# Folding the maxima to 64 partitions on VectorE before they are transposed

## The chip, the cores and the metric

The kernel runs on one NeuronCore of a Trainium2 chip. The metric is the device time of one execution in microseconds (us). Three executions of the kernel before took 636.18, 636.55 and 637.14 us; their median, 636.55 us, is the time before.

A word on the engines, as the profile names them: PE is TensorE (its weight loads are listed apart, as PEld), DVE is VectorE, ACT is ScalarE, POOL is GpSimd, SP is SyncE, which here issues most DMAs. Each works off its own queue in order; semaphores tie them together.

## What is computed

One layer of a diffusion backbone for 1024 tokens of width 1024, and 256 context tokens. A normalised, modulated input goes through one projection; half of its columns feed a neighbourhood attention (8 heads of 64, a clamped window of 8 by 16 grid cells and a learned bias, with all 256 context keys in the same softmax), the other half a gated short convolution; one output projection follows. The change touches the softmax of the attention alone:

```
s_lat = einsum(q_rot, k_rows) * scale + bias        # masked outside the window
s_ctx = einsum(q_plain, kc) * scale
s = concatenate([s_lat, s_ctx], axis=-1)
p = softmax(s, axis=-1)
o = einsum(p_lat, v_rows) + einsum(p_ctx, vc)
```

The softmax subtracts a maximum over all keys of a query. That maximum is what the changed lines work out.

## The kernel before

The kernel has four parts: the modulation and the normalised input (to about 78 us), the projection of queries, keys and values (to about 265 us), the attention, and the output projection (from about 533 us). The change lies in the attention.

**How the attention is tiled.** Scores are kept transposed, with the keys on the 128 partitions and the queries along the free dimension. Queries come in 8 blocks of 128, keys likewise; a block j of keys meets the query blocks j - 1 to j + 1, up to 384 columns. The 256 context keys are two further blocks. The loop at the end calls `quarter(n)` for n from 0 to 35: four quarters for each of the eight heads, each with 256 queries, and some more to let the pipeline run empty. A quarter works at three depths at once: it takes the scores of quarter n, the exponentials of quarter e = n - 2, and the product with the values of quarter o = n - 3.

**The maximum of a query.** `mx` is one tile of 128 partitions by 1024 queries. `ctx_max` (L992) writes the maximum of the two context blocks into the 256 columns of a quarter, `lat_max` (L1007) takes the maximum with the biased scores `sb` of a key block, in place, twice a quarter. After that each column of `mx` holds 128 partial maxima, one for each partition. They are brought together over the partitions two quarters after their scores, in `quarter` (L1082 to L1097): TensorE transposes the two blocks of 128 columns into a PSUM tile `pm` (`pmx` in the profile), VectorE reduces each over its 128 elements to `rm`, one number for each query; TensorE transposes `rm`, broadcast, back into the other half of `pm`, and ScalarE copies that to `mg`, where all partitions hold the maximum of each query. `ctx_exp` (L1030) and L1111 subtract `mg` from the scores `sc` and `sb`; the exponentials and their low parts (`phc`, `plc`, `phl`, `pll`) follow.

**What sets the order.** From the list `strict` on, every instruction on TensorE, ScalarE, VectorE and GpSimd is chained behind the one issued before it on its engine, so that the attention's instructions stand just as the program writes them. Between the attention's own matmuls TensorE runs fillers: matmuls of the gates and of the convolution (`pu`), handed out in ticks by the table `TICKS`. On VectorE, the splits `ul` of the filler's weights, the gates and the convolution's products stand between `rm` and `sc`, where the maximum is on its way through TensorE and ScalarE. So a quarter on VectorE reads: `rm`, fillers' work, `sc`, `sb` less `mg`, the new `sb` with its bias, `mx` from context, `mx` twice from `sb`, `pll`; then the next quarter's `rm`. On TensorE: the pair of transposes of `mx`, the context's product with the values (`po`, six matmuls), the pair of transposes of `rm`, the scores `pss` and `pc`, fillers, `po` of the window, fillers.

Almost every instruction passes through one helper, so the profile shows L55 for them and they are told apart by their tiles.

Of the kernel before, what the change touches and what calls it, by code (L numbers as in the profile page):

```python
# [14 lines left out]
ALU = mybir.AluOpType  # L15
AX = mybir.AxisListType
# [3 lines left out]
P = 128  # L20
# [19 lines left out]
def body(tc, es, x, ctxt, w_ada, b_ada, w_in, q_g, k_g, rpbr, w_out, vecs, cst, out):  # L40
# [21 lines left out]
    pe, act, dve, pool = every = [ordered(e) for e in (nc.tensor, nc.scalar, nc.vector, nc.gpsimd)]  # L62
# [50 lines left out]
    ident = ci[:, 0:P]  # L113
# [196 lines left out]
    def do_acts():  # L310
        for c in soon + (slow if not any(c[1] and c[1].__name__ == "product" for c in soon) else []):
            if c[0]:
                c[0]()
                c[0] = None

    def do_dves(most=99):
        for queue in chores:
            while queue and not queue[0][0] and (queue is soon or most > 0 and not soon):
                on_dve = queue.pop(0)[1]
                if on_dve:  # L320
                    on_dve()
                    most -= 1
# [481 lines left out]
    for m in range(1, 4):  # L804
        k, new, last = 2 * m, m < 3, m == 3
# [247 lines left out]
    def pair_of(n):  # L1053

        h, g = divmod(n, 4)
        two = [(h, 0), (h - 1, 7)] if g == 0 else [(h, 2 * g - 1), (h, 2 * g)]
        return [(i, heads[h_], j) for i, (h_, j) in enumerate(two) if 0 <= h_ < NH]

    def both(v, n, pair):

        w = 256 if n % 4 == 0 else 384
        return v[:, pair[0][0]:pair[-1][0] + 1, :w]

    def maxima_of(n, pair):

        step, w = (768, 256) if n % 4 == 0 else (P, 384)
        lo = (2 * (n % 4) - 2) * P if n % 4 else pair[0][0] * step
        v = mg[:, lo:lo + w].rearrange("p (o c) -> p o c", o=1)
        if len(pair) == 1:
            return v  # L1070
        part = list(v.ap)
        return bass.AP(v.tensor, v.offset, [part[0], [step, 2], [1, w]])

    def quarter(n):

        live = lambda m: 0 <= m < 4 * NH
        ticks = TICKS[n]  # L1080
        e, o = n - 2, n - 3
        if live(e):  # L1082
            hd, g = heads[e // 4], e % 4
            pm = psm.tile([P, 512], F32, name="pmx", tag="C", bufs=2)
            for i in range(2):
                pe.transpose(pm[:, i * P:(i + 1) * P], mx[:, (2 * g + i) * P:(2 * g + i + 1) * P], ident)
            rm = ap.tile([P, 2], F32, name="rm", tag="rm", bufs=8)
            dve.tensor_reduce(rm, pm[:, :256].rearrange("p (i k) -> p i k", i=2), AX.X, ALU.max)
        if live(o):
            heads[o // 4].ctx_out(o % 4)  # L1090
        do_dves(3)
        if gating and next(gating[0], "end"):
            gating.pop(0)
        if live(e):
            for i in range(2):
                pe.transpose(pm[:, 256 + i * P:256 + (i + 1) * P], rm[:, i:i + 1].broadcast_to([P, P]), ident)
            act.copy(mg[:, g * 256:(g + 1) * 256], pm[:, 256:512])  # L1097
        now = pair_of(n)
        for i, hd_, j in now:
            hd_.scores(j, sbank[:, i])  # L1100
        if n == 0:
            next(fill)
            ticks -= 1
        if live(n):
            heads[n // 4].ctx_scores(n % 4)
        if live(e):
            hd.ctx_exp(g)
        if e in sbs or e in exps:
            pair, sb = pair_of(e), sbs.pop(e)
            w = both(sb, e, pair)  # L1110
            dve.tensor_tensor(w, w, maxima_of(e, pair), ALU.subtract)  # L1111
            exps[e] = [ap.tile([P, 2, 384], F32R, name=m, tag=m, bufs=2) for m in ("phl", "pll")]
            ph, pl = (both(v, e, pair) for v in exps[e])
            act.activation(ph, w, AF.Exp)
            act.activation(w, w, AF.Exp)
        for _ in range(n > 0):
            next(fill, None)
        done = []
        if o >= 0:
            pho, plo = exps.pop(o)  # L1120
            for i, hd_, j in pair_of(o):
                hd_.lat_out(j, pho[:, i], plo[:, i])
                if j in (4, 7):
                    done.append((hd_, j // 7))
                    if j == 7 and hd_.s:
                        ready.append(hd_.p)
        if now:
            sb = sbs[n] = sb_new()
            g_ = n % 4
            if g_:  # L1130
                bt = now[0][1].bt
                bias = bt[:, 1:2].broadcast_to([P, 2, 384]) if g_ == 2 else bt[:, 0:2] if g_ == 1 else bt[:, 1:3]
                dve.tensor_tensor(sb, sbank[:, :, :384], bias, ALU.add)
            else:
                for i, hd_, j in now:
                    cols = slice(P, 384) if j == 0 else slice(0, 256)
                    dve.tensor_tensor(sb[:, i, :256], sbank[:, i, :256], hd_.bt[:, 1, cols], ALU.add)
            if live(n):
                heads[n // 4].ctx_max(n % 4)
            for i, hd_, j in now:  # L1140
                hd_.lat_max(j, sb[:, i])
        if e in sbs or e in exps:
            dve.tensor_tensor(pl, w, ph.bitcast(F32), ALU.subtract)
        for _ in range(ticks - (n > 0)):
            next(fill, None)
        for hd_, bank_ in done:
            hd_.finish(bank_)
        do_acts()
# [36 lines left out]
    for n in range(NT + 3):  # L1185


        p, t = divmod(n, NB)
# [119 lines left out]
    with sbuf("att") as ap, psum("psb") as psb:  # L1308
        sbank = psb.tile([P, 2, 512], F32, name="pss")
        strict[:] = every  # L1310
        mx = ap.tile([P, T], F32, name="mx")
# [3 lines left out]
        for n in range(4 * NH + 4):  # L1315
            h, g = divmod(n, 4)
            if 0 < h < NH and g == 0:
                heads[h].load_v()
            if h + 1 < NH and g:
                nx = heads[h + 1]  # L1320
                for load in ((nx.masks, nx.load_q), (nx.load_k,), ())[g - 1]:
                    load()
            quarter(n)
            if ready:
                p = ready.pop()
                if p < NPAIR - 1:
                    gating.append(gated(p))
                else:
                    recip(p, ap)
# [149 lines left out]
```

## Time and profile before

| | us |
|---|---|
| median of three runs | 636.55 |
| the profiled execution, by the device | 636.67 |
| its span, first to last instruction | 634.9 |
| PE busy in the span | 627.2 |
| DVE busy in the span | 443.2 |
| the reduces `rm` start, first and last of 32 | 279.0 and 513.6 |

The page and the views are of one execution. A row of the timeline gives start, duration, engine, line, operation, output<-inputs, shape (partitions x elements; for a matmul rows*columns of the weights, then what is moved) and count; what stands in square brackets is idle time of the engine just before, and what ended it. A row of the grouped view gives, behind the shapes and the count, busy time and mean duration in ns, then the idle time before the group and its releasers. In the view of one tile the three numbers behind the count are the shortest, median and longest duration in ns. Instructions of one engine overlap a little, so the time from one start to the next can be shorter than a duration.

### The profile page before, as it was taken

How to read it: one execution, taken by the hardware profiler on the slowest of the kernel's cores; microseconds unless marked ns; L12 is line 12 of the kernel's file. 1: busy time of each engine (PE TensorE's matmuls, PEld its weight loads, DVE VectorE, ACT ScalarE, POOL GpSimd, SP SyncE). 2: the span in 40 equal slices, each digit the busy share in tenths (PEclk: the TensorE clock that was granted, in tenths of full speed). 3: DMA queues.
4: the chain of work that ended last, by engine and by line, in shares of the span. 5: the costliest groups of instructions: out<-in, count | busy, mean ns of one | idle time of the engine just before them, and what ended most of it. 6: DMA issues, size and time to landing. Idle time of an engine off the chain costs nothing.

```text
span 634.9 us, 10080 instructions
## 1 busy us (share of the span) xinstructions
PE 627.2 (99%) x3503; PEld 538.8 (85%) x3504; DVE 443.2 (70%) x827; ACT 324.0 (51%) x699; POOL 122.5 (19%) x133
## 2 busy tenths in 40 slices
PE   8999999999999999999999999999999999999998
PEld 3477899999899999888888888888888888888787
DVE  1677858765766845468898889988998964476411
ACT  4676835424624545345576658567775854352000
POOL 1305014123123221101122111111111111002400
DMA  8972638867784994875383636583742233965721
GB/s 322 384 260 97 181 114 263 252 198 219 243 264 137 302 330 159 302 246 177 118 273 114 230 109 205 187 284 101 251 146 75 59 103 117 299 212 177 254 101 50
DMA packets 103007, 125.61 MB, mean 198 GB/s; under 512 B 9665, under 2 KB 71577, under 8 KB 101676
## 3 DMA queue, kind: packets, MB, share of 16 engines
q1 hardware_dynamic: 96492, 113.38, 53.7%
q10 hardware_dynamic: 6208, 11.05, 5.5%
q0 software_dynamic: 256, 0.54, 0.4%
q8 instruction: 27, 0.44, 0.3%
q14 instruction: 24, 0.20, 0.1%
HBM read 88.09 MB, written 38.62 MB: 200 GB/s over the span
## 4 chain that ended last, share of the span: by engine, by line
PE 81%; DVE 9%; DMA 5%; ACT 2%; issue 1%; POOL 0%; ACTq 0%; DVEq 0%; POOLq 0%
PE pu L55 23%; PE pacc L55 21%; PE po L55 7%; PE acc L55 6%; PE tr L55 5%; PE cacc L55 4%; PE pss L55 3%; DMA woraw<-in_w_out 2%; PE pmx L55 2%; DVE mx L55 2%; PE pout L75 2%; PE pout L76 2%; PE pout L74 2%; DMA tb<-y_d 2%; PE pc L55 2%; DVE sb L55 2%
## 5 line engine op out<-in xcount | busy, mean ns | idle before, releaser
L55 PE MATMUL pu<-h,uh 128*128 128x512 f32 x544 | 169.2, 392 | 0.0
L55 PE MATMUL pacc<-wh,h 128*128 128x384 f32 x512 | 135.3, 338 | 0.0
L55 PEld LDWEIGHTS pu<-h,uh 128*128 128x128 f32 x544 | 98.2, 188 | 16.9
L55 PE MATMUL pu<-h,ul 128*128 128x512 f32 x272 | 106.4, 391 | 0.0
L55 PEld LDWEIGHTS pacc<-wh,h 128*128 128x128 f32 x512 | 92.9, 188 | 0.1
L55 PE MATMUL pacc<-wl,h 128*128 128x384 f32 x256 | 85.7, 335 | 0.0
L55 POOL TENSOR_TENSOR plc<-sc,phc 128x512 fp32r<-128x512 f32 x32 | 43.0, 1345 | 215.7 <-ACT sc L55 159.1
L55 POOL TENSOR_TENSOR ss<-ss,few 128x4 f32<-128x4 f32 (+1 forms) x40 | 41.4, 1037 | 126.3 <-DVE ss L55 126.1
L55 DVE TENSOR_TENSOR mx<-mx,sb 128x384 f32<-128x384 f32 (+1 forms) x64 | 59.4, 937 | 2.0
L55 PEld LDWEIGHTS pu<-h,ul 128*128 128x128 f32 x272 | 51.1, 188 | 11.2
L75 PE MATMUL pout<-wol,yh 128*128 128x512 f32 (+1 forms) x136 | 51.4, 378 | 0.2 <-DVE wol L1358 0.2
L76 PE MATMUL pout<-woh,yl 128*128 128x512 f32 (+1 forms) x136 | 50.8, 377 | 0.0
L74 PE MATMUL pout<-woh,yh 128*128 128x512 f32 (+1 forms) x136 | 49.9, 378 | 0.0
L55 PEld LDWEIGHTS pacc<-wl,h 128*128 128x128 f32 x256 | 48.2, 188 | 0.1
L55 DVE TENSOR_REDUCE ss<-sq 128x4 f32<-128x260 f32 (+1 forms) x40 | 15.7, 394 | 42.2 <-ACT sq L55 42.2
L55 ACT ACTIVATE sq<-pacc 128x256 f32<-128x256 f32 x32 | 12.3, 384 | 54.7 <-PE pacc L55 54.2
L55 ACT COPY mg<-pmx 128x256 f32<-128x256 f32 x32 | 11.9, 372 | 52.0 <-PE pmx L55 45.6
L55 ACT COPY sc<-pc 128x512 f32<-128x512 f32 x32 | 18.8, 588 | 25.6 <-PE pc L55 25.6
L55 DVE TENSOR_TENSOR pll<-sb,phl 128x768 fp32r<-128x768 f32 (+2 forms) x33 | 28.4, 861 | 4.5 <-ACT sb L55 4.5
L55 ACT ACTIVATE qn<-pacc,ss 128x64 f32<-128x64 f32 x128 | 30.0, 329 | 3.0 <-issue 2.5
L55 PE MATMUL po<-phl,v 128*65 128x256 f32 (+2 forms) x160 | 31.3, 291 | 0.0
L75 PEld LDWEIGHTS pout<-wol,yh 128*128 128x128 f32 x136 | 25.6, 188 | 5.3 <-DVE wol L1358 0.6
(156 smaller groups left out, 1259.5 us busy)
## 6 DMA issues: line engine op xcount, KB each, us to landing
uraw<-in_w_in SPq DMA_DIRECT2D x34, 256.0 KB
q_d<-qs SPq DMA_DIRECT2D x32, 256.0 KB
k_s<-k_d SPq DMA_DIRECT2D x8, 1024.0 KB
q_s<-q_d SPq DMA_DIRECT2D x16, 512.0 KB
wr<-in_w_in SPq DMA_DIRECT2D x40, 192.0 KB
slab<-in_w_ada SPq DMA_DIRECT2D x6, 1024.0 KB
v_d<-vs SPq DMA_DIRECT2D x20, 260.0 KB
v<-v_d SPq DMA_DIRECT2D x16, 325.0 KB
```

The lines of the kernel that those rows point to most:

```text
L55: i = emit(*a, **kw)
L74: i = pe.matmul(ps, ah, bh, start=first, stop=False)
L75: pe.matmul(ps, ah, bl, start=False, stop=False)
L76: pe.matmul(ps, al, bh, start=False, stop=last)
```

## The change

The two transposes of `mx` read 64 partitions instead of 128, with a 64 by 64 corner of the identity, and write 64 columns each; the reduce reads 2 by 64 elements instead of 2 by 128 for each partition. For that, a new instruction on VectorE, at the end of the maxima of each quarter n, takes the 256 columns of the quarter before, whose maxima are complete by then, and writes the larger of partitions 0 to 63 and 64 to 127 into partitions 0 to 63, in place.

```diff
             for i in range(2):
-                pe.transpose(pm[:, i * P:(i + 1) * P], mx[:, (2 * g + i) * P:(2 * g + i + 1) * P], ident)
+                pe.transpose(pm[:, i * 64:(i + 1) * 64], mx[0:64, (2 * g + i) * P:(2 * g + i + 1) * P], ident[:64, :64])
             rm = ap.tile([P, 2], F32, name="rm", tag="rm", bufs=8)
-            dve.tensor_reduce(rm, pm[:, :256].rearrange("p (i k) -> p i k", i=2), AX.X, ALU.max)
+            dve.tensor_reduce(rm, pm[:, :P].rearrange("p (i k) -> p i k", i=2), AX.X, ALU.max)
...
             for i, hd_, j in now:
                 hd_.lat_max(j, sb[:, i])
+        if live(n - 1):
+            low, high = (mx[64 * i:64 * i + 64, (n - 1) % 4 * 256:(n - 1) % 4 * 256 + 256] for i in range(2))
+            dve.tensor_tensor(low, low, high, ALU.max)
         if e in sbs or e in exps:
             dve.tensor_tensor(pl, w, ph.bitcast(F32), ALU.subtract)
```

The built program shows where the new instruction falls. On DVE, this is one quarter of the loop before, from one reduce to the next (a row gives the operation, the tiles, the shape of the output, and the semaphores that it waits for):

```order
L55 TENSOR_REDUCE rm<-pmx 128x2 [waits PE_49]
L55 TENSOR_TENSOR ul<-uraw,uh 128x512 [waits DMAHW7_49,Activation_49]
L55 TENSOR_TENSOR ul<-uraw,uh 128x512 [waits DMAHW2_49,Activation_49]
L55 TENSOR_TENSOR sc<-sc,mg 128x512 [waits Activation_49,Pool_49]
L55 TENSOR_TENSOR sb<-sb,mg 128x768
L55 TENSOR_TENSOR sb<-pss,bt 128x768 [waits DVE_49,PE_49]
L55 TENSOR_TENSOR mx<-pc,sc 128x256 [waits Activation_49]
L55 TENSOR_TENSOR mx<-mx,sb 128x384 [waits DVE_49] x2
L55 TENSOR_TENSOR pll<-sb,phl 128x768 [waits Activation_49]
L55 TENSOR_REDUCE rm<-pmx 128x2 [waits PE_49]
```

And the end of the same quarter in the changed program:

```order
L55 TENSOR_TENSOR sb<-pss,bt 128x768 [waits DVE_49,PE_49]
L55 TENSOR_TENSOR mx<-pc,sc 128x256 [waits Activation_49]
L55 TENSOR_TENSOR mx<-mx,sb 128x384 [waits DVE_49] x2
L55 TENSOR_TENSOR mx<-mx 64x256 [waits DVE_49]
L55 TENSOR_TENSOR pll<-sb,phl 128x768 [waits DVE_49,Activation_49]
L55 TENSOR_REDUCE rm<-pmx 128x2 [waits PE_49]
```

The new maximum stands between the second `mx` from `sb` and `pll`, and both it and `pll` now wait for the DVE instruction before them.

On PE, the piece of the difference that holds the transposes of one quarter and what follows them:

```order
-L55 MATMUL pmx<-ci,mx 128x128 [waits DVE_49,Activation_49]
-L55 MATMUL pmx<-ci,mx 128x128 [waits DVE_49]
+L55 MATMUL pmx<-ci,mx 128x64 [waits DVE_49,Activation_49]
+L55 MATMUL pmx<-ci,mx 128x64
 L55 MATMUL pmx<-ci,rm 128x128 [waits DVE_49]
 L55 MATMUL pmx<-ci,rm 128x128
```

The transposes stay where they were and wait for DVE as before, the first of the pair for both; that of `rm` is unchanged. No other instruction moves on any engine.

## The prediction

> **What bounds the kernel now.** I read the page's busy times first, then the stage that the change touches, then its waits, then one quarter of it in order of time.
>
> ```profile
> span 634.9 us, 10080 instructions
> PE 627.2 (99%) x3503; PEld 538.8 (85%) x3504; DVE 443.2 (70%) x827; ACT 324.0 (51%) x699; POOL 122.5 (19%) x133
> L55 PE MATMUL pmx<-ci,mx x64: 269/272/328, 278.5 to 513.3; 128*128 128x128 f32 x64
> 273.00:516.00 243.00, 241.12 (x1388) 205.09 (x1388) 213.75 (x321) 156.47 (x261) 41.95 (x37) 1.00 0.51 167
> ```
>
> The second line says TensorE (PE) is busy 99% of the span. The third, from the view of the tile pmx, says that the 64 transposes to be shortened run from 278.5 to 513.3 us, two in each of 32 quarters of the attention loop. The fourth is that stretch alone (columns: stretch, length, busy time of PE, PEld, DVE, ACT, POOL, granted clock, DMA share, GB/s): PE is busy 241.1 of 243 us, VectorE (DVE) 213.75, at full clock. So DVE has 29.3 us idle, 0.9 us a quarter. That average doesn't decide; what counts is whether the idle time lies where the new instruction goes. The waits of the stage:
>
> ```profile
> L55 DVE TENSOR_REDUCE rm<-pmx 128x2 f32<-128x256 f32 x32 | 13.5, 423 | 13.3 <-PE pmx L55 13.0
> L55 DVE TENSOR_TENSOR sc<-sc,mg 128x512 f32<-128x512 f32 x32 | 21.9, 685 | 9.8 <-ACT mg L55 9.8
> L55 DVE TENSOR_TENSOR ul<-uraw,uh 128x512 fp32r<-128x512 f32 x25 | 16.8, 684 | 1.9 <-ACT uh L55 1.9
>   PE pmx L55: 13.0, 16
>   DVE rm L55: 4.2, 12
> ```
>
> In a group's row the last part is DVE's idle time ahead of it and its releaser. The last two lines are of the view of the tile rm: its reduce waited for PE in 16 quarters, 13.0 us together, and 12 of the records of PE and PEld waited for the reduce, 4.2 us. In 16 quarters, then, PE sets the pace and DVE has 0.81 us to spare at the reduce; in the other 16 DVE arrives at it without a pause. This is one of the latter:
>
> ```profile
> 347.21 0.42 DVE L55 TENSOR_TENSOR mx<-pc,sc 128x256 f32<-128x256 f32 x1
> 347.66 2.07 DVE L55 TENSOR_TENSOR mx<-mx,sb 128x384 f32<-128x384 f32 x2
> 349.65 0.95 DVE L55 TENSOR_TENSOR pll<-sb,phl 128x768 fp32r<-128x768 f32 x1
> 350.09 0.38 PE L55 MATMUL pmx<-ci,mx 128*128 128x128 f32 x2
> 350.52 0.42 DVE L55 TENSOR_REDUCE rm<-pmx 128x2 f32<-128x256 f32 x1
> 350.89 0.28 PE L55 MATMUL po<-plc,v 128*65 128x256 f32 x1
> 351.01 0.42 PE L55 MATMUL pmx<-ci,rm 128*128 128x128 f32 x2
> 351.46 0.37 ACT L55 COPY mg<-pmx 128x256 f32<-128x256 f32 x1 [1.60 <-PE pmx L55]
> 351.94 0.69 DVE L55 TENSOR_TENSOR sc<-sc,mg 128x512 f32<-128x512 f32 x1 [1.00 <-ACT mg L55]
> 352.55 0.95 DVE L55 TENSOR_TENSOR sb<-sb,mg 128x768 f32<-128x768 f32 x1
> ```
>
> It is a ring. DVE runs from sc through sb, the sums, the maxima (mx) and pll to the reduce (rm) without a gap; the reduce releases PE's second pair of transposes, those ACT's copy mg, that DVE's next sc. The 1.00 us before sc is no spare time: it is the way through PE and ACT, and moves along when the reduce comes late. PE's second pair starts at 351.01, when the reduce has been over for 0.07 us (350.52 + 0.42 = 350.94). Whatever delays the reduce by more than that stops PE, and PE, busy throughout, has nowhere to regain it.
>
> **The change, part by part.** Added, 32 times: a maximum of 64 partitions by 256 elements on DVE, between the last mx and pll, ahead of the reduce. No row has 64 partitions, or two inputs that start on different partitions. The nearest is the same operation on 256 elements in all partitions, mx<-pc,sc, 0.42 us. I take that, since it has the same elements for each partition. Around it lie waits. The order of the changed program shows the maximum waiting for the mx before it, and pll, which so far didn't wait for DVE, waiting for the maximum. Today pll starts before mx is over: 347.66 + 2.07 = 349.73 against 349.65, so 0.08 us of overlap is lost. A DVE instruction that waits for the one before starts 0.03 us after its end (347.21 + 0.42 = 347.63, then 347.66). Together 0.08 + 0.03 + 0.42 + 0.03 = 0.56 us more before pll, and before the reduce.
>
> [...]
>
> Shortened: the reduce reads 128 elements instead of 256. Its nearest row has 130:
>
> ```profile
> L55 DVE TENSOR_REDUCE ss<-sq 128x2 f32<-128x130 f32 x8 | 2.3, 289 | 15.3 <-ACT sq L55 15.3
> 14.36 0.41 PE L55 MATMUL tr<-ci,rw 2*128 2x2 f32 x4 [0.23 <-DVE xss L55]
> L55 PE MATMUL tr<-ci,rw x16: 194/198/222, 14.4 to 62.1; 2*128 2x2 f32 x8, 4*128 4x4 f32 x8
> ```
>
> 423 - 289 = 134 ns, so 0.14 us off (a little more for 128). The ring grows by 0.56 - 0.14 = 0.42 us a quarter on DVE.
>
> Shortened too: each first transpose moves 64 columns instead of 128. Today two follow each other in 0.38 - 0.27 = 0.11 us. The bound from below is a transpose of 2 columns: four take 0.41 us and one 0.20, so (0.41 - 0.20) / 3 = 0.07 us each. Half of 0.11 is 0.055, under that bound; I take 0.07. That gives 0.04 us a transpose, 0.08 a quarter.
>
> [...]
>
> Now the quarters. Sixteen have the reduce straight behind pll: each passes 0.42 us on to PE, 16 × 0.42 = 6.7 us. They don't feel the shorter transposes. Of the sixteen with idle time five have 0.26 to 0.36 us, 1.5 us together; these are the first and the last:
>
> ```profile
> 285.41 0.42 DVE L55 TENSOR_REDUCE rm<-pmx 128x2 f32<-128x256 f32 x1 [0.36 <-PE pmx L55]
> 427.42 0.42 DVE L55 TENSOR_REDUCE rm<-pmx 128x2 f32<-128x256 f32 x1 [0.27 <-PE pmx L55]
> ```
>
> They pay 5 × 0.42 - 1.5 = 0.6 us. The other eleven hide it all in DVE's idle time (13.0 - 1.5 = 11.5 us, about 1 us each), and there PE gains 0.08 us: -0.9 us. Were that cover gone, they would pay 11 × 0.42 = 4.6 us more. Last, DVE's 1.9 us ahead of ul (waiting for ACT's uh, not for the ring) can take up lateness: -1.9 us, if all of it lies in late quarters. Sum: 6.7 + 0.6 - 0.9 - 1.9 = 4.5 us.
>
> ACT, POOL and SP get nothing new, and no DMA moves. What lies behind a late reduce is named above: PE's transposes, and behind them on PE the scores pss and pc and all fillers; so ACT's mg and DVE's sc are late next. POOL stops DVE's maxima for a moment today,
>
> ```profile
> 347.43 1.30 POOL L55 TENSOR_TENSOR plc<-sc,phc 128x512 fp32r<-128x512 f32 x1 [5.94 <-PE po L55]
> ```
>
> but plc ends at 348.73, and the two mx (2.07 us for two that take 1.15 in 275.73) at 349.73, so the new maximum starts clear of it.
>
> ```profile
> 275.73 1.15 DVE L55 TENSOR_TENSOR mx<-mx,sb 128x384 f32<-128x384 f32 x2
> ```
>
> Bounds for the price that no row shows. From below: 0.29 us, the row of 130 elements, as if half the partitions took half the time. The ring then grows by 0.29, and 16 × 0.29 - 16 × 0.08 - 1.9 = +1.4 us. From above: 0.69 us, the row of 512 elements (sc), as if the two halves were read one after the other. The ring grows by 0.69, and 11.0 + (5 × 0.69 - 1.5) - 0.9 - 1.9 = +10.2 us.
>
> The profiled execution took 636.67 us by the device (span 634.9 and 1.8 around it), 0.1 over the median of 636.55. 636.67 + 4.5 = 641.2; against the median 641.0.
>
> **The rivals.**
>
> *The cover holds (faster).* DVE's 29.3 us of idle time exceed 32 × 0.42 = 13.4 us, and PE, the busiest engine, loses 32 × 0.08 = 2.6 us of work: 634.0. For it: PE waits for the reduce only 4.2 us in the whole stage. Against it: the quarter at 347 us, where DVE pauses nowhere but in the ring's way through PE and ACT. It decides if the maximum costs the ring less than the 0.07 us that PE has at its second pair, which no row suggests.
>
> *A wash.* The maximum at its lower bound, +1.4 us, with somewhat more lateness taken up by ACT's and PE's queues: 637.2, in reach of what counts as no change. For it: 64 partitions are half of every row seen. Against it: all DVE rows go by elements a partition (256: 0.42, 512: 0.69, 768: 0.95).
>
> *DVE becomes the bound.* At the upper bound, or if the eleven covered quarters lose their cover because every quarter begins late: 641.0 + 4.6 = 645.6, up to 636.6 + 10.2 = 646.8. For it: a late quarter begins the next one late. Against it: lateness that comes through PE moves PE and DVE alike and leaves the idle time before the reduce as it is.
>
> That the change doesn't do what it says is excluded as far as the order goes: 32 maxima are there, and 64 transposes write 64 columns.
>
> **How the numbers follow.** Forecast, DVE's ring lengthened where DVE arrives last, 639.0 to 643.5 by itself: 0.68. A wash: 0.14. Cover holds: 0.08. DVE the bound: 0.10. A measurement of this kernel tells about 0.2%, 1.3 us, from no change, so under 635.3 is faster and over 637.8 slower. Slower: 0.68 + 0.10 + a fifth of the wash, 0.81. Same: 0.11. Faster: 0.08. For 8 in 10 the range goes from 637.2 (the wash, all below left out) to 645.0 (most of the third rival left out).
>
> **What would show it.** Right: mx<-mx 64x256 at 0.42 us, and pll starting 0.03 us after it; rm at 0.29 us; two transposes in 0.07 us; DVE's wait for pmx before the reduce well under 13.0 us, PE's waits for rm above 4.2 us and in more than 12 records. The quarters with 0.6 us and more of idle time keep their length, those without grow by about 0.4. Wrong: PE's waits for rm unchanged (cover held), a maximum far from 0.42 us, or one stretched by plc; a shift that arises outside 279 to 516 us.

## The result, and the profile after

Four executions of the changed kernel took 645.5 us in the median (644.83 to 646.01), four of the kernel before beside them 636.61 us (636.18 to 637.14): the ratio is 1.0139, interval 1.0126 to 1.0151. The kernel became slower, as forecast, by 8.9 us where 4.5 were forecast, and 0.5 us beyond the top of the range. The profiled execution is the fastest of the four, 644.83 us, 8.2 us over the profiled one of before.

The page of the changed kernel starts with span and busy times; behind the dots are three stretches, the middle one being the attention (columns as before: stretch, length, busy time of PE, PEld, DVE, ACT, POOL, granted clock, DMA share, GB/s).

```profile
span 643.0 us, 10142 instructions
PE 632.6 (98%) x3503; PEld 536.3 (83%) x3504; DVE 457.4 (71%) x859; ACT 324.3 (50%) x699; POOL 122.2 (19%) x133
...
0.00:273.00 273.00, 270.45 (x1575) 237.44 (x1577) 175.16 (x428) 137.07 (x389) 63.67 (x81) 1.00 0.72 237
273.00:525.00 252.00, 247.20 (x1390) 202.73 (x1389) 227.44 (x353) 156.58 (x261) 42.35 (x37) 1.00 0.50 162
525.00:643.00 118.00, 114.94 (x543) 96.11 (x540) 54.77 (x80) 30.62 (x50) 16.22 (x15) 1.00 0.49 169
```

The two outer stretches of the kernel before:

```profile
0.00:273.00 273.00, 270.42 (x1576) 237.70 (x1578) 175.45 (x428) 136.82 (x389) 63.73 (x81) 1.00 0.72 238
516.00:634.90 118.90, 115.63 (x543) 95.97 (x541) 53.98 (x80) 30.67 (x50) 16.78 (x15) 1.00 0.51 168
```

Until 273 us the two agree. The attention went from 243.0 to 252.0 us, the rest from 118.9 to 118.0. The clock is full in all of them. So the whole loss arises where the change lies. DVE has 13.7 us more to do there (227.44 against 213.75). But PE is busy 6.1 us longer too (247.20 against 241.12), with transposes that were to be shorter, and idle 2.9 us longer (252.00 - 247.20 = 4.8 against 1.9).

The waits of the stage, by group and, in the last two lines, by the tile rm:

```profile
L55 DVE TENSOR_TENSOR ul<-uraw,uh 128x512 fp32r<-128x512 f32 x25 | 16.8, 684 | 1.5 <-ACT uh L55 1.5
L55 DVE TENSOR_TENSOR mx<-mx 64x256 f32<-64x256 f32 x32 | 16.5, 517 | 1.1
L55 DVE TENSOR_REDUCE rm<-pmx 128x2 f32<-128x128 f32 x32 | 9.2, 287 | 5.4 <-PE pmx L55 5.3
  PE pmx L55: 5.3, 8
  DVE rm L55: 4.5, 15
```

The reduce waits for PE in 8 quarters and 5.3 us, where it did in 16 and 13.0: the new maximum (the fold, from here on) has used up the idle time. The records that wait for the reduce went from 12 and 4.2 us to 15 and 4.5, the idle time ahead of ul from 1.9 to 1.5. Almost nothing of this looks like 8.9 us, since a ring that turns more slowly shows its waits in no single place.

One wait has become longer. These are the groups of the first transposes, before and after:

```profile
L55 PE MATMUL pmx<-ci,mx 128*128 128x128 f32 x64 | 12.7, 275 | 0.7 <-DVE mx L55 0.7
L55 PE MATMUL pmx<-ci,mx 64*128 64x64 f32 x64 | 10.3, 240 | 4.2 <-DVE mx L55 2.1 <-ACT z L55 0.7 <-ACT ob L55 0.7
```

PE's idle time ahead of them grew from 0.7 to 4.2 us. They wait for DVE as before, but for a later instruction: until now for the maxima of the turn, now for the fold behind them. In the quarter of the prediction the last of these maxima was over at 349.73 us, and the pair started at 350.09 without a pause; after, the fold is over at 353.44 and the pair starts at 353.59. That isn't what makes the reduce of this quarter late: it follows pll at 354.42 without idle time, is over at 354.70, and the second pair starts at 354.76, 0.06 us behind it where it was 0.07. What the longer wait costs elsewhere, no run isolates.

The length of the ring is read better from the start of one reduce to the start of the next. Reduces around the quarter of the prediction, before and after:

```profile
343.33 0.42 DVE L55 TENSOR_REDUCE rm<-pmx 128x2 f32<-128x256 f32 x1 [0.83 <-PE pmx L55]
...
357.81 0.42 DVE L55 TENSOR_REDUCE rm<-pmx 128x2 f32<-128x256 f32 x1 [0.65 <-PE pmx L55]
```

```profile
346.46 0.29 DVE L55 TENSOR_REDUCE rm<-pmx 128x2 f32<-128x128 f32 x1 [0.24 <-PE pmx L55]
...
354.42 0.28 DVE L55 TENSOR_REDUCE rm<-pmx 128x2 f32<-128x128 f32 x1
...
361.61 0.29 DVE L55 TENSOR_REDUCE rm<-pmx 128x2 f32<-128x128 f32 x1
```

Before, the reduce between these two starts at 350.52 (shown with the prediction). So the quarter that ends in a late reduce went from 350.52 - 343.33 = 7.19 to 354.42 - 346.46 = 7.96 us, by 0.77 rather than 0.42; the one behind it, which had 0.65 us of idle time, from 7.29 to 7.19. Done for all 31 distances, this gives a table, with the forecast's terms and some of the experiments below (us, sums over the quarters of a kind; the kinds are those of the kernel before). A reduce belongs to the distance that it begins, so what a shorter reduce saves shows in the quarter behind it:

| quarters | forecast | after | fold_only | fold_rows65 | extra64 |
|---|---|---|---|---|---|
| 16 with no idle time at the reduce | 6.7 - 1.9 | +8.25 | +8.56 | +7.40 | +3.25 |
| 5 with 0.26 to 0.36 us | +0.6 | +1.27 | +1.47 | +0.86 | +1.43 |
| 10 with 0.64 us and more | -0.9 (of 11) | -0.96 | -0.07 | -2.33 | +2.66 |
| all, first reduce to last | | +8.56 | +9.96 | +5.93 | +7.34 |

### The profile page after: what moved, and what is told of

Read it like the earlier page. It is cut to its first block, busy times and chain, and to the rows that moved or that the text cites. A ratio compares the mean times of both kernels' runs of the same rounds, so it can differ in the third digit from the quotient of the medians.

```text
span 643.0 us, 10142 instructions
## 1 busy us (share of the span) xinstructions
PE 632.6 (98%) x3503; PEld 536.3 (83%) x3504; DVE 457.4 (71%) x859; ACT 324.3 (50%) x699; POOL 122.2 (19%) x133
## 4 chain that ended last, share of the span: by engine, by line
PE 89%; DVE 7%; ACT 2%; issue 2%; POOL 0%; ACTq 0%; DVEq 0%; POOLq 0%
PE pu L55 23%; PE pacc L55 21%; PE po L55 7%; PE acc L55 7%; PE tr L55 5%; PE pout L76 5%; PE pout L74 5%; PE pout L75 5%; PE cacc L55 4%; DVE mx L55 3%; PE pmx L55 3%; PE pss L55 2%; PE pc L55 2%; DVE sb L55 2%; PE trA L55 1%
## 5 line engine op out<-in xcount | busy, mean ns | idle before, releaser
L55 DVE TENSOR_TENSOR mx<-mx,sb 128x384 f32<-128x384 f32 (+1 forms) x64 | 58.1, 916 | 2.0
L1409 DVE TENSOR_TENSOR ot<-pout,xr 128x512 f32<-128x512 f32 (+1 forms) x9 | 5.7, 632 | 34.6 <-PE pout L76 32.9
```

Source lines behind the costliest of these rows:

```text
L55: i = emit(*a, **kw)
L1409: dve.tensor_tensor(ot[:, c], ps[c.start // 256][:, c], xr[:, c], ALU.add)
```

## The experiments

Three theories stood at the start. A: the ring on DVE grew about as forecast, and the transposes of 64 rows, instead of saving PE 0.08 us a quarter, cost it some 0.19. B: the transposes save as forecast, and the fold alone is dearer than it looks. C: the fold is hidden after all, and only the transposes cost.

What raised A were two pieces of PE's timeline. Before:

```profile
349.85 0.39 PE L55 MATMUL pu<-h,ul 128*128 128x512 f32 x1
350.09 0.38 PE L55 MATMUL pmx<-ci,mx 128*128 128x128 f32 x2
350.22 0.48 PE L55 MATMUL po<-phc,v 128*65 128x256 f32 x2
350.54 0.28 PE L55 MATMUL po<-plc,v 128*65 128x256 f32 x1
```

and after:

```profile
360.92 0.39 PE L55 MATMUL pu<-h,ul 128*128 128x512 f32 x1
361.24 0.33 PE L55 MATMUL pmx<-ci,mx 64*128 64x64 f32 x2
361.51 0.46 PE L55 MATMUL po<-phc,v 128*65 128x256 f32 x2
361.80 0.28 PE L55 MATMUL po<-plc,v 128*65 128x256 f32 x1
```

From the last filler's start to the first plc matmul's it was 350.54 - 349.85 = 0.69 us, and is 361.80 - 360.92 = 0.88. Half the columns, and 0.19 us more. Each transpose is shorter (median 232 ns for 272). But the two still start 0.11 us apart, and the time lies at the borders: filler to pair 0.32 instead of 0.24, and pair to the plc matmul 0.56 instead of 0.45. The second piece is from the quarter behind the one of the first, since PE waits ahead of the pair there; the distance is 0.87 or 0.88 us in 16 quarters of the changed kernel, those in which the pair follows the filler in 0.32.

**fold_only.** The fold stays, the transposes and the reduce are as before.

```diff
-                pe.transpose(pm[:, i * 64:(i + 1) * 64], mx[0:64, ...], ident[:64, :64])
+                pe.transpose(pm[:, i * P:(i + 1) * P], mx[:, ...], ident)
-            dve.tensor_reduce(rm, pm[:, :P].rearrange("p (i k) -> p i k", i=2), AX.X, ALU.max)
+            dve.tensor_reduce(rm, pm[:, :256].rearrange("p (i k) -> p i k", i=2), AX.X, ALU.max)
```

> The change without its savings: the new maximum on VectorE stays, the transposes read 128 partitions and write 128 columns again, the reduce reads 256 elements. Theory A (the change costs twice: VectorE's ring grows by the maximum and its waits, and the 64-row transposes cost TensorE 0.19 us a quarter instead of saving 0.08): the ring grows by 0.63 us (0.42 plus 0.03, 0.10 and 0.08 of waits and lost overlap), about 9 to 10 us slower than before, so as slow as the change or a little slower, since the shorter reduce is gone as well. Theory B (the transposes save as forecast and the maximum alone is dearer than forecast): slower than the change by the lost savings, 11 us or more over before. Theory C (only the transposes cost, the maximum is covered): within 1 us of before.

Measured: 646.8 us (646.65 to 647.69), ratio 1.0156 (1.0143 to 1.017) to a kernel before of 637.05: +9.75. The fold by itself costs more than the whole change. C has fallen: were the fold hidden, this would have been no slower than before. PE's busy time alone would have misled: it grew here too, with the old transposes, to 245.28 us from 273 to 526.3 us, 4.2 more than before.

**fold_halfred.** The fold and the shorter reduce, transposes of 128 rows and columns.

```diff
+                pe.transpose(pm[:, i * P:(i + 1) * P], mx[:, ...], ident)
+            dve.tensor_reduce(rm, pm[:, :256].rearrange("p (i k) -> p i k", i=2)[:, :, :64], AX.X, ALU.max)
```

> The maximum on VectorE and the reduce over 64 elements of each block stay; the transposes read 128 partitions and write 128 columns as before. Theory A: 6 to 7 us over before, 2 us under the change. Theory B: 10 us or more over before, slower than the change. Theory C: within 1 us of before.

Measured: 643.16 us (642.57 to 643.38), ratio 1.0095 (1.0081 to 1.0108): +6.1. So the shorter reduce is worth 9.75 - 6.1 = 3.6 us, and the full transposes, put back into the change, make it 8.9 - 6.1 = 2.8 us faster (2.3 by the two medians as they stand, whose kernels before differ by 0.4). B has fallen too.

**fold_rows65.** The whole change, with one row and one column more in each transpose.

```diff
+                pe.transpose(pm[:, i * 65:(i + 1) * 65], mx[0:65, ...], ident[:65, :65])
+            dve.tensor_reduce(rm, pm[:, :130].rearrange("p (i k) -> p i k", i=2), AX.X, ALU.max)
```

> The whole change, but the transposes read 65 partitions and write 65 columns (the reduce reads 65). [...] Theory A, if the cost on TensorE comes from going to a 64-row tile and back: the pair is 0.27 us a quarter quicker than in the change, 5 to 6 us over before. If it comes from the few columns (a weight load that no longer hides): as slow as the change, 9 us over before. Theory B: as slow as the change.

Measured: 642.64 us (642.13 to 642.9), ratio 1.0087 (1.0073 to 1.0101): +5.6. The same piece of PE's timeline:

```profile
360.77 0.39 PE L55 MATMUL pu<-h,ul 128*128 128x512 f32 x1
361.00 0.28 PE L55 MATMUL pmx<-ci,mx 65*128 65x65 f32 x2
361.10 0.43 PE L55 MATMUL po<-phc,v 128*65 128x256 f32 x2
361.36 0.28 PE L55 MATMUL po<-plc,v 128*65 128x256 f32 x1
```

361.36 - 360.77 = 0.59 us: 0.10 less than before, where the forecast had 0.08 less, and 0.29 less than with 64 rows. One more row and one more column make PE faster. This kernel is what the forecast described, and it comes out 1.1 us above it.

**fold_same_rows.** fold_only, with a fold that reads and writes the same 64 partitions, which changes nothing in them; pll then has one wait less.

```diff
-            dve.tensor_tensor(low, low, high, ALU.max)
+            dve.tensor_tensor(low, low, low, ALU.max)
```

> As the first kernel, but the maximum takes partitions 0 to 63 with themselves, so that it changes nothing, its two inputs start on the same partition and the instruction after it needs no wait. Theory A: the maximum itself takes 0.42 us as before, and the wait and the lost overlap behind it (0.18 us) go: about 3 us less than the first kernel, 6 us over before. If the wait costs nothing beyond the instruction itself: equal to the first kernel.

Measured: 643.02 us (642.04 to 643.72), ratio 1.0093 (1.0079 to 1.0107): +6.0, and 3.8 us less than fold_only. DVE's timeline in fold_only,

```profile
353.31 0.42 DVE L55 TENSOR_TENSOR mx<-mx 64x256 f32<-64x256 f32 x1
353.83 0.96 DVE L55 TENSOR_TENSOR pll<-sb,phl 128x768 fp32r<-128x768 f32 x1
```

and in fold_same_rows:

```profile
352.42 0.42 DVE L55 TENSOR_TENSOR mx<-mx 64x256 f32<-64x256 f32 x1
352.77 0.94 DVE L55 TENSOR_TENSOR pll<-sb,phl 128x768 fp32r<-128x768 f32 x1
```

Fold and pll last equally long. Where pll waits for the fold it starts 0.52 us after the fold's start, 0.10 after its end; without that wait 0.35, which is 0.07 before its end. The operand in the other half of the partitions costs nothing that shows in the fold's duration, 0.42 us in both.

**extra65** and **extra64.** These put the question of the rows to the kernel before by itself: one idle transpose a quarter more, between the pair and po, into columns of the PSUM tile that mg's transposes write over later. The two differ by one row and one column.

```diff
+            pe.transpose(pm[:, 256:256 + 65], mx[0:65, 2 * g * P:(2 * g + 1) * P], ident[:65, :65])
```

> The kernel before with one idle transpose more in each quarter, of 65 partitions and 65 columns, between the pair of mx and the product po; its result is overwritten. It measures TensorE alone, VectorE's work is as before. It occupies TensorE for 0.06 us, 32 times 0.06 = 1.9 us, less what falls into TensorE's idle time: 1 to 2 us over before, whatever the theory.

> The same with 64 partitions and 64 columns. Theory A (going to a 64-row tile and back costs TensorE 0.2 to 0.25 us beside the transpose itself): 32 times 0.3 = 9 to 10 us on TensorE, of which 1 to 2 fall into its idle time, so 7 to 9 us over before, and the neighbours of the transpose start about 0.1 us late on both sides. If 64 rows cost nothing of their own: equal to the kernel with 65.

Measured: extra65 637.77 us (637.1 to 639.67), ratio 1.0012 (1.0001 to 1.0023), +0.9 to a kernel before of 636.87; extra64 644.56 us (643.53 to 645.04), ratio 1.0118 (1.0097 to 1.0138), +7.7. One transpose, 6.8 us apart. In the timeline of extra65 (the profile counts the three transposes in one row, with the shape of the first):

```profile
351.12 0.39 PE L55 MATMUL pu<-h,ul 128*128 128x512 f32 x1
351.35 0.44 PE L55 MATMUL pmx<-ci,mx 128*128 128x128 f32 x3
351.60 0.43 PE L55 MATMUL po<-phc,v 128*65 128x256 f32 x2
351.87 0.28 PE L55 MATMUL po<-plc,v 128*65 128x256 f32 x1
```

and in extra64:

```profile
352.20 0.39 PE L55 MATMUL pu<-h,ul 128*128 128x512 f32 x1
352.43 0.58 PE L55 MATMUL pmx<-ci,mx 128*128 128x128 f32 x3
352.94 0.45 PE L55 MATMUL po<-phc,v 128*65 128x256 f32 x2
353.23 0.28 PE L55 MATMUL po<-plc,v 128*65 128x256 f32 x1
```

the filler lies 0.75 and 1.03 us ahead of plc: 0.28 us between 65 rows and 64, much as between the two forms of the change (0.29).

**extra64x2.** extra64 with two such transposes in a row.

```diff
+            for _ in range(2):
+                pe.transpose(pm[:, 256:256 + 64], mx[0:64, 2 * g * P:(2 * g + 1) * P], ident[:64, :64])
```

> Two of the transposes of 64 partitions in a row. If the price is one for going there and back, the second adds only its own 0.06 to 0.11 us: 2 to 3.5 us more than with one. If each 64-row transpose pays by itself: 7 us more or above.

Measured: 645.52 us (645.45 to 646.18), ratio 1.0133 (1.0115 to 1.015): +8.7, only 1.0 us over extra64, about what extra65 costs over the kernel before. So the price, (7.7 - 0.9) / 32 = 0.21 us, is paid for each trip from matmuls of 128 rows to one of 64 by 64 and back, and not for each such transpose. Whether the 64 rows or the 64 moved columns are to blame, these runs don't separate, since rows and columns change together.

**pll_late, after_pll_late, rows65_pll_late.** An attempt to take the fold out of the reduce's way: pll, on which the reduce doesn't depend, moves behind it in every quarter, in the kernel before, in the change and in fold_rows65.

```diff
+        while late:
+            late.pop()()
...
-            dve.tensor_tensor(pl, w, ph.bitcast(F32), ALU.subtract)
+            late.append(lambda: dve.tensor_tensor(pl, w, ph.bitcast(F32), ALU.subtract))
```

> The kernel before with one instruction moved: VectorE computes pll behind the reduce rm instead of ahead of it, that is, in the time in which the maximum is on its way through TensorE and ScalarE. Theory A (VectorE's ring from rm to rm sets the pace in about half of the quarters): the ring loses 0.87 us, TensorE's 4.2 us of waits for rm go in large part, 2 to 3 us faster than before. If VectorE's ring doesn't bind: within 1 us of before; if pll now delays sc in the quarters that have fillers' work in that gap: slower than before.

> The changed kernel with the same move. Theory A: with the ring shorter by 0.87 us the new maximum and its waits (0.63 us) are hidden, and what is left is TensorE's loss at the 64-row transposes, 32 times 0.19 = 6 us, on top of the time of the kernel before with this move: 3 to 4 us over before. If the transposes cost nothing of their own: equal to the kernel before with this move, or 1 us less (the shorter reduce).

> The change with 65 partitions transposed, and the same move of pll. Theory A: the maximum is hidden, and TensorE has 32 times 0.09 = 2.9 us less work than in the kernel before with this move: 5 to 6 us faster than before, the quickest of all. If the maximum isn't hidden: as slow as the kernel before with this move, or slower.

Measured: 639.76 us (638.99 to 640.84), 647.54 (647.01 to 649.67) and 643.83 (642.66 to 646.23), ratios 1.004 (1.0025 to 1.0054), 1.0166 (1.0147 to 1.0185) and 1.0097 (1.0081 to 1.0113) to 637.28. That is +2.5, +10.3 and +6.5 us: in all three theory A missed, and none is faster than the kernel that it was made from. In pll_late the reduce shows why:

```profile
L55 DVE TENSOR_REDUCE rm<-pmx 128x2 f32<-128x256 f32 x32 | 13.6, 425 | 29.9 <-PE pmx L55 29.9
...
  PE pmx L55: 29.9, 32
```

Now it waits for PE in all 32 quarters, 29.9 us instead of 13.0. What pll did while PE got its transposes ready is done behind the reduce instead, in DVE's idle time ahead of sc, which falls from 9.8 to 1.5 us; in many quarters the fillers' work already filled DVE until sc, and there sc is put off.

With the fold there is a second reason: the pair of transposes needs the fold, and the reduce needs the pair, so the fold stays in the ring wherever pll goes. PE's waits for DVE ahead of the pair, in pll_late (for the maxima) and in rows65_pll_late (for the fold), as total, times and longest:

```profile
PE pmx L55 <- DVE mx L55: 1.8, 7, 0.5
PE pmx L55 <- DVE mx L55: 9.4, 14, 1.4
```

**pll_late_six.** The kernel before, with the move in six quarters only, those where DVE came last and had little between rm and sc.

```diff
+LATE = [3, 5, 8, 19, 27, 31]
...
+            if n in LATE:
+                late.append(low_part)
+            else:
+                low_part()
```

> The kernel before with pll behind rm in six quarters alone (pll of quarters 3, 5, 8, 19, 27 and 31), in which VectorE came last and had little or nothing to do between rm and sc. Theory A: the ring loses 0.87 us there and nothing is pushed back, about 1.4 us (0.2%) faster than before; in the other 26 quarters the move cost more than it gave. If the ring doesn't bind in these quarters: as before; if the move is bad everywhere: slower.

Measured: 635.17 us (634.05 to 637.06), ratio 0.9973 (0.9962 to 0.9985): 1.7 us faster than the kernel before, where the move in all quarters made it 2.5 us slower. The view of the tile rm:

```profile
  PE pmx L56: 13.6, 21
  DVE rm L56: 1.5, 3
```

The records that wait for the reduce fall from 12 and 4.2 us to 3 and 1.5, and the reduce waits hardly longer for PE (13.6 us for 13.0). Where the pause lies decides, not how much of it there is.

## Why the prediction was right and wrong

**The ring** was right. The loss lies in the attention, in the quarters without idle time at the reduce, and DVE's pauses elsewhere didn't help. Those quarters grew by 8.25 / 16 = 0.52 us on average where 0.42 were forecast, before any slack. The cover-holds rival (634.0) has fallen with fold_only, and the wash with it.

**The fold's price** was right: 420 ns at the least and 421 in the median, for 0.42 forecast. (The lower bound of this price adds up to +1.5 us rather than +1.4, a slip on which nothing here depends.) Its mean of 517 comes from three that fell under POOL's plc, which the forecast had excluded; the first of them:

```profile
453.45 0.76 DVE L55 TENSOR_TENSOR mx<-mx,sb 128x256 f32<-128x256 f32 x2
454.25 1.53 DVE L55 TENSOR_TENSOR mx<-mx 64x256 f32<-64x256 f32 x1
...
454.20 1.30 POOL L55 TENSOR_TENSOR plc<-sc,phc 128x512 fp32r<-128x512 f32 x1 [7.59 <-ACT sc L55]
```

That cost next to nothing: in the kernel before the mx of this quarter was held up in its place,

```profile
447.24 1.86 DVE L55 TENSOR_TENSOR mx<-mx,sb 128x256 f32<-128x256 f32 x2
```

so the work up to the fold's end went from 1.86 to 454.25 + 1.53 - 453.45 = 2.33 us, by 0.47, what the fold takes with the wait ahead of it.

**The waits around it** were undersized. The forecast had pll start 0.03 us after the fold; it started 0.10 after (fold_only's rows above), so the ring grew by 0.63 instead of 0.56 before the reduce, 16 × 0.07 = 1.1 us. The 0.03 is that of an instruction that waits for DVE alone (in the kernel before, the mx behind the one from context starts 0.03 or 0.04 us after it in all 32 quarters). But pll waits for ACT as well, and the changed program has 62 instructions more, not 32 (10142 for 10080; fold_same_rows, where pll waits for ACT alone, has 10112). The other 30 are waits by themselves on DVE. One stands between the fold and pll: in the quarter at 353 us it starts 0.04 us after the fold, lasts 0.02, and pll starts 0.04 after it.

**The reduce** was right (284 ns for 0.29).

**The slack ahead of ul** failed: of the 1.9 us that were to take up lateness, 0.4 went. Most of it stands in one quarter, in the kernel before

```profile
444.04 0.69 DVE L55 TENSOR_TENSOR ul<-uraw,uh 128x512 fp32r<-128x512 f32 x1 [1.43 <-ACT uh L55]
```

and after:

```profile
450.26 0.69 DVE L55 TENSOR_TENSOR ul<-uraw,uh 128x512 fp32r<-128x512 f32 x1 [0.93 <-ACT uh L55]
```

A pause takes up the growth of its own quarter, here 0.50 us, and no more, since what it waits for comes later by all that the quarters before have lost. The forecast had let one pause pay for several quarters. Another pause, which its sum didn't have, helped as much: in the quarter that begins at 387.43 us ACT was busy with other work and started mg only 2.55 us after the reduce; in the changed kernel it is 1.96 us, and the quarter is 8.80 us long instead of 8.91.

**The first transposes** failed, and this is the largest miss: "That gives 0.04 us a transpose, 0.08 a quarter." PE lost 0.19 us a quarter there instead, and without that loss the time lies within the range (fold_rows65, 642.64 us). The price was taken from the distance between two transposes of the same shape, two rows of 128 and four of 2 rows, and a stay in one shape doesn't show what it costs to get there from a filler of 128 rows and back to po. With 65 rows the saving is there as forecast (0.10). In fold_rows65 the ten covered quarters become 2.33 us shorter, 0.23 each, more than the transposes' 0.10; what else is shorter there is the reduce ahead of them, which the forecast had counted in the late quarters alone (fold_halfred, with the old transposes, has these ten 1.39 us shorter, 0.14 each). The changed kernel has 0.96 left of that, near the forecast's -0.9 only by coincidence: the 64 rows take back more than half. Of the 4.4 us between forecast and result, 8.9 - 5.6 = 3.3 are the 64 rows; the other 1.1 is what fold_rows65 lies above the forecast. That it is only 1.1 is partly luck: the waits (1.1) and the slack ahead of ul (1.5) were each short by more than the 0.5 us by which the range was missed, and pauses that the sum left out, like the one at 387 us, took some of it back.

Where the 64 rows cost time is seen against fold_halfred. Its quarter that goes with the one of 7.96 us:

```profile
346.11 0.29 DVE L55 TENSOR_REDUCE rm<-pmx 128x2 f32<-128x128 f32 x1 [0.17 <-PE pmx L55]
346.62 0.38 PE L55 MATMUL pmx<-ci,rm 128*128 128x128 f32 x2
353.93 0.28 DVE L55 TENSOR_REDUCE rm<-pmx 128x2 f32<-128x128 f32 x1
```

and the second pair in the changed kernel:

```profile
347.11 0.38 PE L55 MATMUL pmx<-ci,rm 128*128 128x128 f32 x2
```

With the old transposes the quarter takes 353.93 - 346.11 = 7.82 us, and the second pair starts 0.51 us after the reduce (0.50 in the kernel before); with 64 rows it takes 7.96, and the pair starts 347.11 - 346.46 = 0.65 us after. So 0.14 us of this quarter's growth are the 64 rows, and six quarters without idle time, all behind a reduce that had waited for PE, show the same: they grow by 0.74 to 0.77 us, in fold_halfred by 0.59 to 0.62. In seven others, behind a late reduce, the two kernels agree within 0.01 us: there the second pair follows the reduce closely (0.34 us after its start in six of them, in both kernels), and the 64 rows don't show. Against fold_rows65 the changed kernel loses 0.85 us in the 16 quarters without idle time, and 0.41 and 1.37 in the other five and ten: most of it where PE sets the pace.

The step lies between 65 rows and 64, with the columns going along: from the filler to plc it is 0.59 us with 65 and 0.88 with 64 in the two forms of the change, 0.75 and 1.03 with the added transpose in the kernel before. A second transpose of 64 rows behind the first costs little more, 1.0 us over 32. The price of a trip is thus some 0.2 to 0.3 us. What TensorE does at the border in this time, no run here shows.

**The third rival** named the time that came (645.6), for another reason: its bounds were a fold of 0.69 us or the loss of all cover, and neither happened. A right number on a wrong mechanism; fold_rows65, where all of that rival's conditions are the same, is at 642.6.

Not tried were 64 moved columns with 128 rows, or more than 64 columns with 64 rows, and a fold of the maxima on TensorE.

## What to carry to other kernels

A matmul of 64 rows among matmuls of 128 is priced with its neighbours: look at the distance from the last matmul of the other shape ahead of it to the first behind it, not at the distance between two of a kind (here the one went from 0.69 to 0.88 us, the other stayed at 0.11). An instruction on an engine that is idle 12% of its time is free only if it stands ahead of one of its pauses in the same turn of the ring (the fold by itself cost 9.75 us here, on a VectorE idle 12% of the attention); list the pauses turn by turn before counting on them. And ask who reads what the new instruction writes: here it was the pair of transposes, and so no move of pll could take the fold out of the ring. The same list shows where a move pays: pll behind the reduce in all quarters cost 2.5 us, in six chosen ones it gained 1.7.

## What the runs showed of the hardware

A transpose of 64 rows and columns among matmuls of 128 rows, or a pair of them, cost TensorE 0.28 to 0.29 us more than with 65 in the timeline, on the way there and back (1.03 against 0.75 us in extra64 and extra65, 0.88 against 0.59 in the change and fold_rows65); of that 0.21 us reached the end (extra64 against extra65, 6.8 us over 32). A second in a row added 1.0 us over 32 (extra64x2).

A VectorE instruction without a wait for the one before started 0.07 us before that one's end (fold_same_rows), one that waited for it alone 0.03 us after (the prediction's row at 347.66), and one that waited for it and for another engine 0.10 us after (fold_only). Between the first and the last lie 0.17 us, and 3.8 us over 32 quarters.

A VectorE maximum with both inputs in SBUF that started under GpSimd's plc was held until plc was over: it ended 0.28 to 0.29 us after plc with 256 columns (the fold above: 454.25 + 1.53 = 455.78 against 454.20 + 1.30 = 455.50) and 0.41 to 0.42 us after with 384, in all 61 cases of the two kernels, 0.14 us less than it took alone (0.42 and 0.56). The maximum from context, which has one input in PSUM, was not held: it took its 0.42 us under plc too, in all eight cases of the two kernels (one at 454.49 us in the kernel before).
